# A hybrid encoder layer on one core: one rule for the PSUM banks of successive blocks, and other numbers of plain row blocks at the front of five blocks

## The chip, the cores and the metric

The kernel runs on one core of a Trainium2 chip. The metric is the device time of one execution in microseconds; before the change the median of three runs is 1933.54 (1931.85 to 1934.7). A profile is one more execution, taken by the hardware profiler; its span goes from the first to the last instruction.

## The reference, cut to what matters

One layer for 256 tokens of width 4096, all in float32. Cut to its shape:

```python
proj = rms_norm(x, g_mix) @ w_in                 # 4096 x 11840, split into eight parts
y_a = latent_attention(q latent, kv latent, rotary key) # 16 heads, dense softmax
y_a = rms_norm(y_a, g_out_mla) * silu(gate_a)
y_b = dilated_mixture_attention(q_b, k_b, v_b)   # 16 heads, ALiBi, three patterns
y_b = rms_norm(y_b, g_out_dil) * silu(gate_b)
x = x + concat(y_a, y_b) @ w_out                 # 4096 x 4096
x = x + (p @ w_ple) * sigmoid(rms_norm(x, g_ple) @ w_ple_gate)   # 4096 x 4096
return rms_norm(x, g_final)
```

Nearly all of the work is in the three large weight matrices, each read once.

## The kernel before, in words

**Products.** Every float32 operand is split into two parts, `hi` and `lo`, that TensorE takes in a faster format, and each product is the sum of three matmuls: activations `hi` by weights `hi` (L133), `hi` by `lo` (L134), `lo` by `hi` (L135). So L134 is the first that needs the weights' `lo`. The activations stand transposed in SBUF (tiles `A...`, `B...`, `T...`) and are loaded into the array, the weights stream through it. A product's result of 128 tokens by 512 columns fills one of the eight PSUM banks, named `m0` to `m3`, `s`, `o`, `t0`, `t1`.

**Weights.** SyncE issues the transfers of weight rows (L796 and L1339) into four `raw` buffers. ScalarE makes `hi` (L115), VectorE makes `lo` (L116), into a ring of tiles: three of the pool `wp` and, by block, one to three tiles that are free at that time (`B4`, `B6`, `Ah2`, ...). A step's conversion begins when the step that last used its ring place has run.

**Blocks.** A weight slice of 1024 columns by 4096 rows is a `Block` (class at L769). It works on two tiles of 128 tokens and two halves of 512 columns. A row block of 128 weight rows is either *plain* (`plain_step`: four products into the banks `M2`, `X`, `M3`, `M4`, 12 matmuls), or two row blocks together form a *fast group* after Strassen and Winograd (`fast_steps`: seven products instead of eight, 21 matmuls, into `M1`, `M2`, `M3`, `M5`, `M7`, `M6`, `M4`, in four steps). The fast groups need extra sums and differences of the operands: VectorE subtracts weights for them (L820) and converts the results (L116, L835). When the last fast group has run, a `mid` task reads the banks `M1`, `M6`, `M7`, `M5`; when the whole block has run, a `done` task reads `M2`, `X`, `M3`, `M4`. Eight banks serve one block, so the next block's first plain row block begins in banks that the `mid` task has read, if the tags are chosen so.

**Which banks.** `tags` gives a block's banks in the order `M2, X, M3, M4, M1, M5, M6, M7` (`Block.NAMES`). Before the change three orders are written out by hand: `EVEN`, `ODD` and `LAST`, and one more for the second block of the dilated group.

**The order of steps.** `weave(fast, lead, trail)` writes the order of a block: `lead` plain row blocks, then each fast group with the other plain row blocks spread among the groups, then `trail` plain row blocks. With `n` groups, 32 - 2n - lead - trail plain row blocks stand within. `lay` appends these steps to one list. The main loop goes through this list; for each step it issues the conversions some steps ahead, runs the step's matmuls, spawns the step's task, and lets every running task go one `yield` further (`advance`). Each engine executes its instructions in the order so written. Small jobs (transposes with their evacuation, attention heads, statistics) are such tasks; they take a bank for transposes by `turn_bank`, in turn from a list that `only` sets.

**The sequence.** Four chunks of the latents (banks by `banks()`, which alternates between `m0, m1` and `m2, m3`); the gate block (first group, 7 fast groups); the rest of that gate with the latent attention's up projections; six blocks of the dilated group's q, k, v; four gate chunks beside the dilated attention; three wide output blocks (`WIDE_O`, 4, 7 and 6 fast groups) and two output chunks; three wide blocks of the last gate (6, 7 and 7 fast groups) and the last chunks.

**Output blocks.** `out_done` (L922) adds the last four banks to the residual (L927), and then, after two yields, squares the result and turns it (`x1_turn`, L726): four transposes into one bank (L734), a yield, and `split_rows`, which reads that bank with ScalarE (L125) and VectorE (L127); four such sets a block. The banks for the turning are `t0, t1` during the first output block, `m0, m1` during the second, `m2, m3` during the third.

**The dilated group.** `d_mid` reads with L676 and L673, `d_done` with L691. **The last gate.** `wide_done` adds the last four banks (L1031) and then works by yields on its quarters: tanh on ScalarE (L1035), two VectorE instructions (L1038, L1039), a square on ScalarE (L1042). **The latents.** `done_a` of the fourth chunk computes the statistics (L357 to L362 and `rsqrt_mean`, L223 to L231) by yields during the gate block.

Of the kernel before, what the change touches and what calls it, by code (L numbers as in the profile page):

```python
# [29 lines left out]
OFF_GA = Q_LORA + KV_LORA + ROPE  # L30
# [48 lines left out]
def encoder_layer(ctx: ExitStack, tc: tile.TileContext, x, p, positions, g_mix, w_in, g_q_latent, w_uq,  # L79
# [3 lines left out]
    x, p, out = x[0], p[0, 0], out[0]  # L83
# [222 lines left out]
    T7 = {}  # L306
# [350 lines left out]
    def d_mid(key, blk):  # L657
        def task():
            tags = D_TAGS[key]
            if len(tags) == 2:  # L660
                d = [slot(b, [NT, 512]) for b in tags]
            else:
                both = slot(tags[0], [2, NT, 512])
                d = [both[:, 0], both[:, 1]]
            D[key] = d
            if key == ("v", 1):
                E["d"] = slot("T5", [2, NT, S])
                nc.gpsimd.dma_start(E["d"], c_dist)
            ps = blk.ps
            sc = [(rxq if key[0] == "q" else rx)[:, t:t + 1] for t in range(NT)]  # L670

            def add(h, t, m, old):
                nc.vector.scalar_tensor_tensor(d[h][:, t], ps[m], sc[t], old, op0=ALU.mult, op1=ALU.add)  # L673

            for t in range(NT):
                nc.scalar.activation(d[0][:, t], ps["M1"], AF.Copy, scale=sc[t])  # L676
            for t in range(NT):
                add(1, t, "M6", d[0][:, t])
            add(0, 1, "M7", d[1][:, 1])
            add(1, 0, "M5", d[1][:, 0])  # L680
            add(1, 1, "M5", d[0][:, 1])
            flags.add(("mid", key))
            yield
        return task

    def d_done(key, blk):
        def task():
            d = D[key]
            sc = [(rxq if key[0] == "q" else rx)[:, t:t + 1] for t in range(NT)]
            for m, t, h in (("M2", 0, 0), ("X", 1, 1), ("M3", 0, 1), ("M4", 1, 0)):  # L690
                nc.vector.scalar_tensor_tensor(d[h][:, t], blk.ps[m], sc[t], d[h][:, t], op0=ALU.mult, op1=ALU.add)  # L691
            if key == ("v", 1):
                E["t"] = slot("T4", [2, NT, S])
                for h in range(HEADS):
                    waiting.append((set(), attend(
                        h, lambda t, h=h: d_cols("q", h)[:, t], lambda t, h=h: d_cols("k", h)[:, t], None,
                        d_cols("v", h), yb_rows(h), True), 2 + h % 2))
                spawn(y_stats(1))
                spawn(split_ya())
            yield  # L700
        return task
# [54 lines left out]
    WP = ["wp"] * 3  # L756
# [165 lines left out]
    def out_done(k, blk):  # L922
        def task():
            quarters = ((0, 0, "M2"), (1, 1, "X"), (0, 1, "M3"), (1, 0, "M4"))
            for t, h, m in quarters:
                xc = x1[2 * k + h][:, t]
                nc.vector.tensor_tensor(xc, xc, blk.ps[m], op=ALU.add)  # L927
            yield
            yield
            turns_ = [x1_turn(2 * k + h) for h in range(2)]  # L930
            for h in range(2):
                for t in range(NT):
                    c = 2 * k + h
                    nc.scalar.activation(junk, x1[c][:, t], AF.Square, accum_out=ss1[:, t, c:c + 1])
                yield from turns_[h]
        return task
# [202 lines left out]


    M = ("m0", "m1"), ("m2", "m3")
    turn = [0]

    def banks():
        turn[0] ^= 1
# [13 lines left out]
    for i in range(4):  # L1159
        add(from_x(400 * i, 400, done_a(i)))  # L1160
    hooks = {}
    EVEN, ODD = ("m0", "m1", "s", "o", "m2", "m3", "t0", "t1"), ("m2", "m3", "t0", "t1", "m0", "m1", "s", "o")
    LAST = "m2", "m3", "s", "o", "m0", "m1", "t0", "t1"

    def weave(fast, lead, trail, e=0):

        n = len(fast)
        inner, out, given = 32 - 2 * n - lead - trail, "c" * lead, 0  # L1170
        for i in range(n):
            k = inner * (i + 1) // n - given
            given += k
            out += "c" * (k - 1) + "s" + "c" * (k > 0) + "sss"
        out += "c" * trail
        if e:
            out = out[:len(out) - trail + e] + "ee" + out[len(out) - trail + e:]
        rest = [kt for kt in range(32) if kt // 2 not in fast]
        return [("fast", j) for j in fast] + [("plain", kt) for kt in rest], out

    def lay(blk, order, mid, done, ple=None, after=(), used={}):

        pairs, shape = order
        step = {"s": iter([x for kind, j in pairs if kind == "fast" for x in blk.fast_steps(j)]),
                "c": iter([x for kind, kt in pairs if kind == "plain" for x in blk.plain_step(kt)]), "e": iter(ple or ())}
        last = shape.rindex("s")
        for i, key in enumerate(shape):
            x = next(step[key])
            x.ring = WP + list(after) if after != () and i > last else blk.ring
            if key == "s":  # L1190
                x.flag = used.get(shape[:i + 1].count("s") / 4)
            if i == last:
                x.after = mid
            if i == len(shape) - 1:
                x.after = done
            steps.append(x)

    def hook(at, f):
        assert at not in hooks
        hooks[at] = f  # L1200
# [6 lines left out]
    x0_s, z0 = {}, {}  # L1207
# [9 lines left out]
    def x_pair(j):  # L1217
# [1 line left out]

    hook(24, lambda: spawn(add_sums(7, x_pair, z0_dst, ("T2", "T3"), "x0_sums", x0_s, 2)))  # L1220
    gated_rings = {("T4", "T7"): ("used", 5), "B4": ("gated", 2), "Al1": ("y_sums", FAST_O - 1), ("T5", "T6"): "kpe"}
    order = weave(range(7), 6, 2)
    blk = Block(w_in[:, OFF_GA:OFF_GA + 1024], lhs_x, x0_s, "x0_sums", order, lambda kt: (), LAST, ("T2", "T3"),
                WP + [("T5", "T6")])
    lay(blk, order, gates_mid(blk), gates_done(blk))
    ga2 = from_x(OFF_GA + 1024, 512, done_gate(0, 2))
    ga2.banks, other = M
    for i in range(8):
        add(ga2, 2 * i, 2 * i + 1)
        add(Chunk(cols(w_uq, 384 * i, 384), 8, 384, lhs_c("q"), other, done_uq(i), lambda j: ["latents"]))  # L1230
# [2 lines left out]
    hook(len(steps), lambda: spawn(y_stats(0)))  # L1233
    hook(len(steps) + 1, lambda: spawn(x_sums()))
    ga3 = from_x(OFF_GA + 1536, 512, done_gate(0, 3))
    ga3.banks = M[0]
    add(ga3)

    x_s = {}
# [2 lines left out]
    def x_sums():  # L1242
# [5 lines left out]
            yield  # L1248
        yield from add_sums(8, x_pair, z, "B0", "x_sums", x_s, first=7)

    for n, key in enumerate((key, i) for i in range(2) for key in "qkv"):
        off = {"q": OFF_Q, "k": OFF_K, "v": OFF_V}[key[0]] + 1024 * key[1]
        order = weave((range(5), range(8), range(8), range(8), (4, 5, 0, 1, 2, 3, 6, 7), (0, 1, 2, 3, 6, 7))[n],
                      16 if n == 0 else 2, 2)
        ring = (["B6", "B4"], ["B4", "B6", "B0"], ["B4", "B6", "B0"], ["B4", "B6"], ["B4", ("T4", "T7")], [("T4", "T7")])[n]
        after = ((), (), ["B4", "B6"], ["B4"], [("T4", "T7")], ())[n]
        tags = LAST if n == 0 else ("t0", "t1", "m2", "m3", "m0", "m1", "s", "o") if n == 1 else (EVEN, ODD)[n % 2]
        blk = Block(w_in[:, off:off + 1024], lhs_x, x_s, "x_sums", order, lambda kt: (), tags, "B1", WP + ring)
        lay(blk, order, d_mid(key, blk), d_done(key, blk), after=after, used={2: ("used", 5)} if n == 4 else {})
    beside = [len(steps), len(steps) + 64]  # L1260
    for c in range(4):
        if c == 3:
# [2 lines left out]
        ch.banks = M[c % 2]  # L1265
        add(ch)

    for k in range(WIDE_O):
        hook(len(steps), only(*(("t0", "t1"), ("m0", "m1"), ("m2", "m3"))[k]))
        for h in range(2):  # L1270
            hook(len(steps) + 4 + h, lambda c=2 * k + h: load_res(c))
        order = weave(*((range(4), 12, 4), (range(7), 4, 4), (range(6), 6, 4))[k])
        blk = Block(w_out[:, 1024 * k:1024 * (k + 1)], lhs_y, y_s, "y_sums", order, lambda kt: need_y(kt // 2),
                    (EVEN, ODD)[k % 2], "Al2" if k < 2 else "Al1", WP + (["Ah2", "Al1"] if k < 2 else [("B7b", "T7")]))
        lay(blk, order, out_mid(k, blk), out_done(k, blk))
    for c in (6, 7):
        hook(len(steps), lambda c=c: (load_res(c), only("t0", "t1")()))
        if c == 7:
            hook(len(steps) + 6, lambda: spawn(x1_sums()))
            hook(len(steps) + 11, lambda: spawn(load_p()))  # L1280
        add(Chunk(cols(w_out, 512 * c, 512), 32, 512, lhs_y, ("m2", "m3") if c == 6 else ("m0", "m1"), done_o(c), need_y))
# [5 lines left out]
                     lambda j: ["pT"])  # L1287

    for k in range(WIDE):
        order = weave(*((range(6), 6, 4) if k == 0 else (range(7), 6, 4)), 2)  # L1290
        blk = Block(w_ple_gate[:, 1024 * k:1024 * (k + 1)], lhs_x1, x1_s, "x1_sums", order,
                    lambda kt: [("x1T", kt // 4)], LAST, "B6", WP + ["B4"])
        lay(blk, order, wide_mid(k, blk), wide_done(k, blk), wide_ple(k))
# [226 lines left out]
```

## Time and profile before

| | |
|---|---|
| median of three runs | 1933.54 us |
| the profiled execution | 1934.57 us |
| its span | 1932.8 us |
| granted TensorE clock | 0.997 |
| VectorE busy | 1560.3 us (81%) |
| ScalarE busy | 1103.9 us (57%) |
| weights' transfers, SyncE's queue | 363.90 MB, 61.5% of the 16 engines' time |

Blocks in the trace, by their first and last plain row block's matmuls: the gate block 156.6 to 241.8, the first two blocks of the dilated group from 491.5 and 580.0, the three output blocks from 1207.3, 1292.7 and 1381.6, the wide blocks of the last gate from 1557.0, 1647.5 and 1736.3.

How to read it: PE is TensorE's matmuls, PEld its weight loads, DVE VectorE, ACT ScalarE, SP SyncE. A timeline row has the start, the duration, the engine, the line, the operation, what it writes and reads, and in brackets how long the engine was idle before it and who ended that. The duration of a matmul is from its start to its modelled end; the next one starts earlier. `L116 ... lo<-raw,hi 128x1024` is the conversion of one row block.

### The profile page before, as it was taken

How to read it: one execution, taken by the hardware profiler on the slowest of the kernel's cores; microseconds unless marked ns; L12 is line 12 of the kernel's file. 1: busy time of each engine (PE TensorE's matmuls, PEld its weight loads, DVE VectorE, ACT ScalarE, POOL GpSimd, SP SyncE). 2: the span in 40 equal slices, each digit the busy share in tenths (PEclk: the TensorE clock that was granted, in tenths of full speed). 3: DMA queues.
4: the chain of work that ended last, by engine and by line, in shares of the span. 5: the costliest groups of instructions: out<-in, count | busy, mean ns of one | idle time of the engine just before them, and what ended most of it. 6: DMA issues, size and time to landing. Idle time of an engine off the chain costs nothing.

```text
span 1932.8 us, 25582 instructions
## 1 busy us (share of the span) xinstructions
PE 1909.9 (99%) x9272; PEld 1626.4 (84%) x9272; DVE 1560.3 (81%) x2162; ACT 1103.9 (57%) x1513; POOL 74.4 (4%) x122
## 2 busy tenths in 40 slices
PE   9999999999999999999999999999999999999997
PEld 8998889998887888888888888887888888888887
DVE  7767966666999999999877778888886688989866
ACT  6555565564655555655556666555555455656543
POOL 1001011220000000000000000000000000000000
PEclk9999999999999999999999999999999999999999
DMA  7666655545666666666665456665666656666675
GB/s 252 189 185 191 201 172 146 148 144 163 192 188 207 198 217 196 209 201 197 213 195 143 132 165 222 207 207 163 222 192 221 189 185 217 191 204 198 208 221 178
DMA packets 147342, 370.59 MB, mean 192 GB/s; under 512 B 12020, under 2 KB 45904, under 8 KB 147216
## 3 DMA queue, kind: packets, MB, share of 16 engines
q1 hardware_dynamic: 145584, 363.90, 61.5%
q0 software_dynamic: 1632, 5.05, 0.7%
q8 instruction: 73, 1.20, 0.3%
q14 instruction: 53, 0.43, 0.1%
HBM read 364.72 MB, written 4.19 MB: 191 GB/s over the span
## 4 chain that ended last, share of the span: by engine, by line
PE 91%; DVE 6%; ACT 1%; DMA 1%; issue 1%; SPq 0%; ACTq 0%; DVEq 0%
PE m L134 20%; PE m L135 19%; PE m L133 19%; PE t L133 3%; PE t L134 3%; PE t L135 3%; PE o L134 3%; PE o L135 3%; PE o L133 3%; PE s L134 3%; PE s L135 3%; PE s L133 3%; DVE lo L116 2%; DVE B L820 1%; DVE B L116 1%
## 5 line engine op out<-in xcount | busy, mean ns | idle before, releaser
L116 DVE TENSOR_TENSOR lo<-raw,hi 128x1024 fp32r<-128x1024 f32 (+4 forms) x502 | 552.1, 1105 | 230.4 <-ACT hi L115 227.6
L115 ACT ACTIVATE hi<-raw 128x1024 fp32r<-128x1024 f32 (+4 forms) x502 | 482.5, 965 | 379.4 <-PE m L135 158.6
L133 PE MATMUL m<-hi,Ah 128*128 128x512 f32 (+2 forms) x1113 | 422.3, 379 | 2.6 <-DVE B L691 1.5
L134 PE MATMUL m<-lo,Ah 128*128 128x512 f32 (+2 forms) x1113 | 417.2, 375 | 0.8 <-DVE lo L116 0.8
L135 PE MATMUL m<-hi,Al 128*128 128x512 f32 (+2 forms) x1109 | 414.6, 374 | 0.0
L133 PEld LDWEIGHTS m<-hi,Ah 128*128 128x128 f32 x1113 | 209.4, 188 | 32.6 <-DVE B L691 2.0
L134 PEld LDWEIGHTS m<-lo,Ah 128*128 128x128 f32 x1113 | 209.5, 188 | 32.4 <-DVE lo L116 3.7
L135 PEld LDWEIGHTS m<-hi,Al 128*128 128x128 f32 x1109 | 208.5, 188 | 32.4 <-DVE Al L127 0.2
L133 PE MATMUL m<-hi,B 128*128 128x512 f32 (+1 forms) x418 | 160.0, 383 | 2.8 <-DVE Al L127 2.8
L134 PE MATMUL m<-lo,B 128*128 128x512 f32 (+1 forms) x418 | 156.5, 374 | 0.2 <-DVE lo L116 0.2
L135 PE MATMUL m<-hi,B 128*128 128x512 f32 (+1 forms) x418 | 156.4, 374 | 0.0
L115 ACT ACTIVATE hi<-B 128x1024 fp32r<-128x1024 f32 x77 | 81.3, 1060 | 83.5 <-DVE B L820 55.2
L116 DVE TENSOR_TENSOR lo<-B,hi 128x1024 fp32r<-128x1024 f32 x77 | 93.8, 1221 | 5.3 <-ACT hi L115 2.8
L133 PEld LDWEIGHTS m<-hi,B 128*128 128x128 f32 x418 | 78.7, 188 | 13.6 <-issue 3.1
L115 ACT ACTIVATE B<-raw 128x1024 fp32r<-128x1024 f32 (+1 forms) x66 | 61.3, 938 | 47.9 <-DMA raw<-in_w_in_dram 18.2
L135 PEld LDWEIGHTS m<-hi,B 128*128 128x128 f32 x418 | 78.8, 188 | 11.7
L134 PEld LDWEIGHTS m<-lo,B 128*128 128x128 f32 x418 | 78.9, 189 | 11.5 <-DVE lo L116 1.0
L820 DVE TENSOR_TENSOR B<-raw,B 128x512 f32<-128x512 f32 x126 | 86.1, 683 | 0.0
L116 DVE TENSOR_TENSOR B<-raw,B 128x1024 fp32r<-128x1024 f32 (+1 forms) x66 | 70.4, 1074 | 16.6 <-ACT B L115 16.5
L116 DVE TENSOR_TENSOR T<-t,T 128x512 fp32r<-128x512 f32 (+1 forms) x65 | 44.4, 683 | 41.6 <-ACT T L115 41.2
L115 ACT ACTIVATE B<-B 128x1024 fp32r<-128x1024 f32 (+1 forms) x58 | 55.5, 957 | 36.6 <-DVE B L820 15.6
L835 DVE TENSOR_TENSOR lo<-raw,hi 128x1024 fp32r<-128x1024 f32 x56 | 68.2, 1218 | 3.6 <-ACT hi L833 3.6
(798 smaller groups left out, 3795.9 us busy)
## 6 DMA issues: line engine op xcount, KB each, us to landing
raw<-in_w_in_dram SPq DMA_DIRECT2D x320, 512.0 KB, 4.0
raw<-in_w_out_dram SPq DMA_DIRECT2D x128, 512.0 KB, 4.5
raw<-in_w_ple_gate_dram SPq DMA_DIRECT2D x128, 512.0 KB, 4.5
raw<-in_w_in_dram SPq DMA_DIRECT2D x63, 400.0 KB, 3.6
raw<-in_w_uq_dram SPq DMA_DIRECT2D x32, 384.0 KB, 3.4
raw<-in_w_ukv_dram SPq DMA_DIRECT2D x16, 512.0 KB, 3.8
T<-in_x_dram SPq DMA_DIRECT2D x7, 512.0 KB, 6.1
T<-in_x_dram POOLq DMA_DIRECT2D x7, 512.0 KB, 7.4
```

The source lines that it names most:

```text
L115: nc.scalar.activation(hi, src, AF.Copy)
L116: nc.vector.tensor_tensor(lo, src, plain(hi), op=ALU.subtract)
L133: nc.tensor.matmul(ps, ah, bh, start=start, stop=False)
L134: nc.tensor.matmul(ps, ah, bl, start=False, stop=False)
L135: nc.tensor.matmul(ps, al, bh, start=False, stop=stop)
L820: nc.vector.tensor_tensor(dst, a, b, op=ALU.subtract)
L835: nc.vector.tensor_tensor(lo, r[1], plain(hi), op=ALU.subtract)
```

## The change

Four things, with no instruction added or taken away:

- A block's banks come from the block in front by one rule, `follow`: the new `M2, X, M3, M4` are the old `M1, M6, M7, M5`, in the order in which the old block's `mid` task reads them; the new `M1, M5, M6, M7` are the old `M2, X, M4, M3`. The dilated group's six blocks and the three output blocks start from `EVEN` and follow on.
- The gate block takes `EVEN` instead of `LAST`, and `banks()` starts with the other pair, so that the `m` banks swap names up to the dilated group.
- `weave`'s lead: the gate block 8 instead of 6, the second output block 6 instead of 4, the third 8 instead of 6, the second and third wide block of the last gate 4 instead of 6.
- `out_done` has one yield less between the additions and the turning.

```diff
@@ out_done
             yield
-            yield
             turns_ = [x1_turn(2 * k + h) for h in range(2)]
@@
-    turn = [0]
+    turn = [1]
@@
-    EVEN, ODD = ("m0", "m1", "s", "o", "m2", "m3", "t0", "t1"), ("m2", "m3", "t0", "t1", "m0", "m1", "s", "o")
+    EVEN = "m0", "m1", "s", "o", "m2", "m3", "t0", "t1"
@@
+    def follow(tags):
+
+        m2, x, m3, m4, m1, m5, m6, m7 = tags
+        return m1, m6, m7, m5, m2, x, m4, m3
@@
-    order = weave(range(7), 6, 2)
-    blk = Block(w_in[:, OFF_GA:OFF_GA + 1024], lhs_x, x0_s, "x0_sums", order, lambda kt: (), LAST, ("T2", "T3"),
+    order = weave(range(7), 8, 2)
+    blk = Block(w_in[:, OFF_GA:OFF_GA + 1024], lhs_x, x0_s, "x0_sums", order, lambda kt: (), EVEN, ("T2", "T3"),
@@
-    ga2.banks, other = M
+    other, ga2.banks = M
@@
-    ga3.banks = M[0]
+    ga3.banks = M[1]
@@
+    tags = EVEN
     for n, key in enumerate((key, i) for i in range(2) for key in "qkv"):
...
-        tags = LAST if n == 0 else ("t0", "t1", "m2", "m3", "m0", "m1", "s", "o") if n == 1 else (EVEN, ODD)[n % 2]
         blk = Block(w_in[:, off:off + 1024], lhs_x, x_s, "x_sums", order, lambda kt: (), tags, "B1", WP + ring)
         lay(blk, order, d_mid(key, blk), d_done(key, blk), after=after, used={2: ("used", 5)} if n == 4 else {})
+        tags = follow(tags)
@@
+    tags = EVEN
     for k in range(WIDE_O):
...
-        order = weave(*((range(4), 12, 4), (range(7), 4, 4), (range(6), 6, 4))[k])
+        order = weave(*((range(4), 12, 4), (range(7), 6, 4), (range(6), 8, 4))[k])
         blk = Block(w_out[:, 1024 * k:1024 * (k + 1)], lhs_y, y_s, "y_sums", order, lambda kt: need_y(kt // 2),
-                    (EVEN, ODD)[k % 2], "Al2" if k < 2 else "Al1", WP + (["Ah2", "Al1"] if k < 2 else [("B7b", "T7")]))
+                    tags, "Al2" if k < 2 else "Al1", WP + (["Ah2", "Al1"] if k < 2 else [("B7b", "T7")]))
         lay(blk, order, out_mid(k, blk), out_done(k, blk))
+        tags = follow(tags)
@@
-        order = weave(*((range(6), 6, 4) if k == 0 else (range(7), 6, 4)), 2)
+        order = weave(*((range(6), 6, 4) if k == 0 else (range(7), 4, 4)), 2)
```

## Prediction

> **What bounds the kernel now.** I read the page's head first, then the waits of TensorE (engine, line, whom it waited for: total us, times, longest us), then the timeline around each of those waits.
>
> ```profile
> span 1932.8 us, 25582 instructions
> PE 1909.9 (99%) x9272; PEld 1626.4 (84%) x9272; DVE 1560.3 (81%) x2162; ACT 1103.9 (57%) x1513; POOL 74.4 (4%) x122
> PE m L133 <- DVE Al L127: 2.8, 1, 2.8
> PE m L133 <- DVE B L691: 1.5, 1, 1.5
> PE m L134 <- DVE B L116: 1.3, 2, 0.7
> PE m L134 <- DVE lo L116: 1.0, 4, 0.4
> PE m L134 <- DVE T L116: 0.6, 1, 0.6
> ```
>
> TensorE is busy for all but 22.9 us, and the change takes no matmul away. So only its waits can go, and these five rows sum to 7.2 us. The busy column hides part of what a wait costs, because a matmul's row (0.39) is longer than the distance between two starts. So I count from start to start:
>
> ```profile
> 1304.60 0.60 PE L734 MATMUL m<-ident,T 128*128 128x128 f32 x4
> 1308.04 0.47 PE L133 MATMUL m<-hi,B 128*128 128x512 f32 x1 [2.85 <-DVE Al L127]
> ...
> 1310.43 0.63 PE L133 MATMUL m<-hi,B 128*128 128x512 f32 x1
> 1310.86 0.63 PE L134 MATMUL m<-lo,B 128*128 128x512 f32 x1
> ...
> 1313.13 0.39 PE L134 MATMUL t<-lo,B 128*128 128x512 f32 x1
> 1313.36 0.40 PE L135 MATMUL t<-hi,B 128*128 128x512 f32 x1
> ```
>
> The undisturbed distance of 512-column matmuls is 0.23 (1313.13 to 1313.36; 0.2266 as a mean over many). Behind the 2.85 us wait eight of them stand 0.43 apart (1310.43 to 1310.86): the array ran at about half speed. A plain row block (4 banks, 12 matmuls) is thus 2.72 us, a fast group (21 matmuls) 4.76, a group with one plain row block in it 7.48.
>
> **The change part by part.**
>
> *Second output block (k = 1): one yield less, six plain row blocks ahead instead of four.* Its first fast product takes bank m0, in which the block in front still turns its result. The four transposes at 1304.60 are that block's third set; the product is issued right behind them and waits until ScalarE and VectorE have read the bank: 3.0 us more than 0.2 between the starts, 1.6 for eight matmuls 0.2 late, 0.2 for the edges: **4.8 us**. With the yield gone the third set stands behind the third plain row block (the order of the changed kernel's instructions shows it), and the product behind the sixth. Three plain row blocks, 8.2 us, lie between; the read took 3.1 (1304.9 to 1308.0). The wait goes whole. What takes its place? The first transposes now follow one plain row block after the last products, 1292.7 + 2.7 = 1295.4, and need the last addition to the result:
>
> ```profile
> 1292.72 0.39 PE L133 MATMUL m<-hi,B 128*128 128x512 f32 x1
> 1292.92 0.69 DVE L927 TENSOR_TENSOR T<-T,o 128x512 f32<-128x512 f32 x1
> ```
>
> It ends at 1293.6, 1.8 us early. The same holds for the other two output blocks. So -4.8. The Trainium skill, "TensorE: Matmul & The Clock Gate", section "Part 1: The HAM clock gate", has the array fall to half clock after at least one idle window of about 3.4 us, and 426.7 ns from start to start there. Those eight distances agree with its rate; a gap of 2.85 us would not fill its window, and by the rule taken strictly the term would be 3.2. The trace shows the slow stretch after this gap, so the rows stand.
>
> *The bank rule at the second block of the dilated group.*
>
> ```profile
> 581.17 0.39 PE L135 MATMUL t<-hi,Al 128*128 128x512 f32 x1
> 583.10 0.50 PE L133 MATMUL m<-hi,Ah 128*128 128x512 f32 x1 [1.53 <-DVE B L691]
> ...
> 582.30 1.40 DVE L691 SCALAR_TENSOR_TENSOR B<-m,st,B 128x512 f32<-128x512 f32 x2
> 584.93 1.21 DVE L116 TENSOR_TENSOR B<-raw,B 128x1024 fp32r<-128x1024 f32 x1
> ```
>
> The third bank of this block's first plain row block was m2, which the block in front fills until its end; VectorE reads it only at 582.3. By the new rule the first four banks are those that were read at the half-way task, done before 580. 1.7 us and 0.1 behind it go: **-1.8**. VectorE works through here without a pause, so what it delivers doesn't come earlier, and the next deadline moves up: the plain row block inside the first fast group is due at 580.04 + 5.44 + 0.68 + 0.23 = 586.4, and its conversion (584.93 + 1.21) ends at 586.15. That just holds; if it is late, by some tenths. At all other block edges of this stretch no wait is listed, and the new rule reads the same four early banks in another order: 0. That the m-banks swap names in front of it changes no distance: 0.
>
> *Gate block of the first group: eight ahead instead of six, so 8 instead of 10 plain row blocks within the seven groups.*
>
> ```profile
> 172.08 1.23 DVE L116 TENSOR_TENSOR lo<-raw,hi 128x1024 fp32r<-128x1024 f32 x1 [2.12 <-ACT hi L115]
> 182.76 1.23 DVE L116 TENSOR_TENSOR T<-raw,T 128x1024 fp32r<-128x1024 f32 x1
> 183.90 0.15 DVE L229 SCALAR_TENSOR_TENSOR st<-st 128x4 f32<-128x4 f32 x1
> ...
> 181.68 0.39 PE L133 MATMUL m<-hi,Ah 128*128 128x512 f32 x1
> 182.43 0.50 PE L134 MATMUL m<-lo,Ah 128*128 128x512 f32 x1 [0.36 <-DVE lo L116]
> ...
> 183.00 0.40 PE L133 MATMUL m<-T,Ah 128*128 128x512 f32 x1
> 184.04 0.50 PE L134 MATMUL m<-T,Ah 128*128 128x512 f32 x1 [0.65 <-DVE T L116]
> ```
>
> The starts lose 0.5 and 0.8, with edges 1.5 us. VectorE is late because the latent's statistics (some 17 small instructions, 2.7 us) fall among its first group. With two more plain row blocks in front, its queue is: conversion of the sixth ends at 173.3 as now, 1.1 for the turned latents, 1.8 for the subtractions and half conversion, 1.1 for the next plain row: 177.3. One group of VectorE there is 7.54 (four subtractions at 0.6, a half conversion at 0.6, four conversions at 1.13) and the statistics 2.7: the second group's plain row is ready at 187.6. TensorE would have wanted it at 184.04 less the 1.5 of waits, and wants it two plain row blocks later: 188.0. After that VectorE needs 7.54 a group against 7.48: level. Here the price is the denser stretch, bounded below by 0 and above by the denser blocks' rows further down (up to 0.9 in one group, so some 1.5). I take 0.1: **-1.4**.
>
> *Wide blocks 1 and 2 of the last gate: four ahead instead of six, 10 instead of 8 within.*
>
> ```profile
> 1702.06 0.39 PE L133 MATMUL m<-B,Ah 128*128 128x512 f32 x1
> 1703.02 0.50 PE L134 MATMUL m<-B,Ah 128*128 128x512 f32 x1 [0.57 <-DVE B L116]
> ...
> 1790.86 0.40 PE L133 MATMUL m<-B,Ah 128*128 128x512 f32 x1
> 1791.97 0.50 PE L134 MATMUL m<-B,Ah 128*128 128x512 f32 x1 [0.71 <-DVE B L116]
> ...
> 1687.31 1.21 DVE L835 TENSOR_TENSOR lo<-raw,hi 128x1024 fp32r<-128x1024 f32 x1
> 1695.14 1.22 DVE L835 TENSOR_TENSOR B<-raw,B 128x1024 fp32r<-128x1024 f32 x1
> 1694.65 5.89 DMA raw<-in_w_ple_gate_dram
> ```
>
> VectorE's group takes 7.83 here (L835 to L835), TensorE's 7.48, so each group loses 0.35, until the fourth and fifth stand still; a weight transfer of 5.89 adds to it. That is 1.0 and 1.2 us. With 10 inside, three groups hold two plain row blocks (10.2 of TensorE) and the loss goes. But the first group now starts 5.4 us earlier, beside the last steps of the block in front:
>
> ```profile
> 1648.26 2.35 DVE L116 TENSOR_TENSOR lo<-raw,hi 128x1024 fp32r<-128x1024 f32 x2
> 1652.66 0.68 DVE L1038 SCALAR_TENSOR_TENSOR B<-B,Q 128x512 f32<-128x512 f32 x1
> 1653.38 0.69 DVE L1039 TENSOR_TENSOR T<-B,T 128x512 f32<-128x512 f32 x1
> ```
>
> Four such pairs, 1.3 to 1.4 each, now stand between the group's conversions. From 1650.6, when the lead is converted: 1.8 for the subtractions, 1.3, until 1654.5 for a transfer, then five conversions (1.14 each), two subtractions (0.6) and three pairs: 1664.3 for the fourth step, due 1664.7. Then 0.5 (the pause before a group's first subtraction in these rows), 1.8, 1.1: 1667.8 against 1666.8. So about 1.0 us of wait comes back, bounds 0 and 1.6 (every pair also late by its own ScalarE input). Net **-0.2** for both.
>
> *Third output block (eight ahead), and the second one's denser middle (8 inside instead of 10 in both).*
>
> ```profile
> 1332.62 1.23 DVE L116 TENSOR_TENSOR lo<-raw,hi 128x1024 fp32r<-128x1024 f32 x1 [0.25 <-ACT hi L115]
> 1336.26 0.39 PE L134 MATMUL m<-lo,B 128*128 128x512 f32 x1
> ```
>
> In the second output block a plain row inside a group is ready 2.4 us ahead of its use (1333.85 to 1336.26), the closest that I found there, since its ring has five places. Five groups at a loss of 0.35 use up 1.8 of it; one slow transfer more uses up the rest. The third output block has two groups in a row at most. I take +0.2, bounds 0 and 1.5.
>
> Sum: -4.8 - 1.8 - 1.4 - 0.2 + 0.2 = **-8.0 us**. The profiled execution took 1934.57 in all (1932.8 of span), 1.0 above the median of the three runs (1933.54): 1926.6 on its own scale, 1925.5 on the median's. I give **1925.6**.
>
> **The rivals.**
> - *The dense middles cost more than the lead gives.* For it: VectorE's 7.83 against 7.48 shows in the rows above, and the removed 4.8 us were also time for VectorE to catch up. In each of the gate block, the second and the third output block up to 1.5 us comes back, and 0.6 more in each wide block: gain 8.0 - 4.5 - 1.2, about 2.5 to 5; 1929 to 1931. Against it: the margins worked out above.
> - *The wide blocks come clean too* (the pairs find gaps): 2.2 instead of 0.2, and nothing at the third output block: gain about 10.2, 1923.3.
> - *Slower.* Mechanism: without the yield the first transposes stand one plain row block behind the last products. If the last addition (L927) ends over 2.7 us after the block's start, TensorE waits there, at three edges. If the wait reaches the 2.85 us of the row above, the half-speed stretch comes with it: 4.8 each, 14.4 in all, less 8.0: 1940. It decides from 1.8 us more delay of that addition; L927 runs 0.9 after the start, and nothing is moved in front of it in VectorE's order.
> - *The rule doesn't do what it says* (a first bank read last somewhere): the 1.8 stays and a second edge like it costs 1.8: 1929.
>
> **How the numbers follow.** The forecast (gain 6.5 to 9.5) 0.55, dense middles 0.19, clean wide blocks 0.13, rule fails 0.07, slower 0.06. The range reaches from a gain of 11 (10.2 and the spread of runs) to one of 3.5: 1922.5 to 1930; it leaves out the slower case and the worst of the dense one. A measurement of this kernel tells about 0.2%, 3.9 us. All cases but the slower and some half of the dense one gain more: faster 0.85, same 0.10, slower 0.05.
>
> **What would show it.** In the changed profile: no wait on L127 and no matmuls 0.43 apart at the second output block; no wait on L691 (its new line) at 580; at 180 to 190 no wait above 0.3; in the wide blocks the wait moves from the fifth group to the second, about 1 us. Wrong would be waits at L734's transposes, growing waits on L116 late in the gate block or the second output block, or a span not shorter by the sum of the waits that went.

## The result and the profile after

The changed kernel takes 1927.40 us (median of 7 runs, 1926.62 to 1928.79); the kernel before, run between them on the same chip, 1933.64 (7 runs). The ratio is 0.997 (95% interval 0.9958 to 0.9981): 6.2 us or 0.3% faster. A second series gave 1927.74 against 1933.52, ratio 0.997 (0.9959 to 0.9981). The execution that was profiled took 1927.64 us. The head of its page and the waits of TensorE (engine, line, whom it waited for: total us, times, longest us):

```profile
span 1925.9 us, 25586 instructions
PE 1909.8 (99%) x9272; PEld 1626.7 (84%) x9272; DVE 1560.8 (81%) x2162; ACT 1101.3 (57%) x1513; POOL 74.5 (4%) x122
```

```profile
PE m L1456 <- DVE junk L1450: 1.5, 1, 1.5
PE m L134 <- DVE lo L116: 0.9, 5, 0.2
PE t L270 <- DMA T<-in_x_dram: 0.9, 1, 0.9
PE t L169 <- DMA T<-in_g_mix_dram: 0.2, 1, 0.2
```

The four instructions more than before (25582) are semaphore instructions, three on VectorE and one on TensorE; the counts of each engine's work are the same.

The waits on L127 (2.8) and L691 (1.5) have no row left, those on L116 fell from 2.9 to 0.9. What stays is at the kernel's start, which no edit aims at, and five small waits of L134. TensorE's busy time moves by 0.1 us only; what went is its idle time, 22.9 us before and 16.1 after.

To see where the time went I cut TensorE's timeline at the first product of each block, and took the distance to the first product of the next one. Every number of a block below is such a length. Before and after, us:

```
                                         before    after    difference
kernel start up to the gate block        156.64   157.19    +0.55
gate block, first group                   85.19    84.21    -0.98
second block of the dilated group         83.42    81.63    -1.79
second output block                       88.87    84.26    -4.61
last gate, second wide block              88.79    88.69    -0.10
last gate, third wide block               88.95    88.59    -0.36
last chunk to its end                     35.46    35.78    +0.32
the 15 others, together                                     +0.04
```

The third output block, whose lead and banks the change alters too, is among the 15: 84.94 before, 84.95 after. The edits bought nothing there.

At the second output block, TensorE's timeline of the changed kernel (start us, length, engine, line, out<-in) shows the third set of transposes and what stands behind it:

```profile
1302.91 0.60 PE L734 MATMUL m<-ident,T 128*128 128x128 f32 x4
1303.26 0.48 PE L133 MATMUL m<-hi,B 128*128 128x512 f32 x1
...
1312.23 0.39 PE L133 MATMUL m<-Al,B 128*128 128x512 f32 x1
1312.46 0.39 PE L134 MATMUL m<-Al,B 128*128 128x512 f32 x1
```

Three plain row blocks follow the set, and nine microseconds on the distance is still 0.23: neither the wait nor the stretch of 0.43 exists. At the start of the second dilated block:

```profile
581.41 0.39 PE L135 MATMUL t<-hi,Al 128*128 128x512 f32 x1
581.63 0.39 PE L133 MATMUL m<-hi,Ah 128*128 128x512 f32 x1
...
583.84 0.74 DVE L691 SCALAR_TENSOR_TENSOR B<-o,st,B 128x512 f32<-128x512 f32 x1
584.50 1.22 DVE L116 TENSOR_TENSOR B<-raw,B 128x1024 fp32r<-128x1024 f32 x1
585.72 0.39 PE L133 MATMUL m<-B,Ah 128*128 128x512 f32 x1
585.94 0.39 PE L134 MATMUL m<-B,Ah 128*128 128x512 f32 x1
```

L691 still reads the old block's banks at 583.8, but the new block's first four banks are others, and TensorE takes the fourth at 581.63 without a gap. The next plain row is met with little to spare: its conversion (L116) ends at 585.72, and the product that needs it starts at 585.94, 0.22 behind the one in front.

In the wide blocks the wait moved to the second group. Before it stood in the fifth and, for the most part, in the sixth, counted from one (the prediction calls them the fourth and fifth):

```profile
1659.06 0.40 PE L133 MATMUL m<-hi,Ah 128*128 128x512 f32 x1
1659.64 0.50 PE L134 MATMUL m<-lo,Ah 128*128 128x512 f32 x1 [0.18 <-DVE lo L116]
1660.20 0.40 PE L133 MATMUL m<-hi,Ah 128*128 128x512 f32 x1
1660.77 0.50 PE L134 MATMUL m<-lo,Ah 128*128 128x512 f32 x1 [0.17 <-DVE lo L116]
```

### The profile page after: what moved, and what is told of

Same layout as the page of the kernel before. It is cut to its first block, busy times and chain, and to the rows that moved or that the text cites. A ratio compares the mean times of both kernels' runs of the same rounds, so it can differ in the third digit from the quotient of the medians.

```text
span 1925.9 us, 25586 instructions
## 1 busy us (share of the span) xinstructions
PE 1909.8 (99%) x9272; PEld 1626.7 (84%) x9272; DVE 1560.8 (81%) x2162; ACT 1101.3 (57%) x1513; POOL 74.5 (4%) x122
## 4 chain that ended last, share of the span: by engine, by line
PE 94%; DVE 4%; DMA 1%; issue 1%; ACT 1%; SPq 0%; DVEq 0%; ACTq 0%
PE m L134 20%; PE m L135 20%; PE m L133 20%; PE t L134 4%; PE t L135 4%; PE t L133 4%; PE s L134 3%; PE o L134 3%; PE o L135 3%; PE o L133 3%; PE s L135 3%; PE s L133 3%; DVE lo L116 1%; PE t L445 1%; DVE B L820 1%
## 5 line engine op out<-in xcount | busy, mean ns | idle before, releaser
L116 DVE TENSOR_TENSOR lo<-raw,hi 128x1024 fp32r<-128x1024 f32 (+4 forms) x497 | 549.0, 1109 | 227.6 <-ACT hi L115 225.0
L133 PE MATMUL m<-hi,Ah 128*128 128x512 f32 (+2 forms) x1130 | 429.2, 380 | 0.0
L134 PE MATMUL m<-lo,Ah 128*128 128x512 f32 (+2 forms) x1130 | 424.6, 376 | 0.9 <-DVE lo L116 0.7
L135 PE MATMUL m<-hi,Al 128*128 128x512 f32 (+2 forms) x1128 | 422.3, 374 | 0.0
L134 PEld LDWEIGHTS m<-lo,Ah 128*128 128x128 f32 x1130 | 212.9, 188 | 34.6 <-DVE lo L116 5.0
L134 PE MATMUL m<-lo,B 128*128 128x512 f32 (+1 forms) x420 | 156.8, 373 | 0.2 <-DVE lo L116 0.2
L135 PE MATMUL m<-hi,B 128*128 128x512 f32 (+1 forms) x420 | 156.7, 373 | 0.0
L116 DVE TENSOR_TENSOR lo<-B,hi 128x1024 fp32r<-128x1024 f32 x75 | 91.6, 1223 | 4.1 <-ACT hi L115 1.8
L134 PEld LDWEIGHTS m<-lo,B 128*128 128x128 f32 x420 | 79.1, 188 | 11.3 <-DVE lo L116 0.9
L116 DVE TENSOR_TENSOR B<-raw,B 128x1024 fp32r<-128x1024 f32 (+1 forms) x66 | 69.4, 1059 | 13.5 <-ACT B L115 13.2
L116 DVE TENSOR_TENSOR T<-t,T 128x512 fp32r<-128x512 f32 (+1 forms) x65 | 44.4, 683 | 41.6 <-ACT T L115 41.2
```

What stands on the lines that cost most here:

```text
L116: nc.vector.tensor_tensor(lo, src, plain(hi), op=ALU.subtract)
L133: nc.tensor.matmul(ps, ah, bh, start=start, stop=False)
L134: nc.tensor.matmul(ps, ah, bl, start=False, stop=False)
L135: nc.tensor.matmul(ps, al, bh, start=False, stop=stop)
```

## Experiments

My theory: the gain is three waits that went, each by its own edit, and the wide blocks gain next to nothing. Against it stood that the edits need each other, that they only move VectorE's delay to another place, and that the output blocks' edges are at the point of tipping over. The tables name lengths as above.

**The lead of the second output block alone** (on the kernel before):

```diff
-        order = weave(*((range(4), 12, 4), (range(7), 4, 4), (range(6), 6, 4))[k])
+        order = weave(*((range(4), 12, 4), (range(7), 6, 4), (range(6), 6, 4))[k])
```

> The kernel before, with only the second output block's lead changed from four plain row blocks to six; both yields stay. My theory: the third set of transposes stays behind the fourth plain row block, the first fast product goes behind the sixth, so 5.4 us of plain work lies where the read of the bank took 3.1: the wait on L127 (2.85 us before) and the eight matmuls 0.43 apart both go, and the block shortens by the whole 4.8 us (88.87 to about 84.0). The rival, that the yield's removal is what frees the bank and the lead only adds cover, has most of the wait left: under 2 us gained. All other blocks unchanged.

Measured: 1929.48 us against 1934.14, ratio 0.9976 (0.9967 to 0.9986). The second output block takes 84.26, to the hundredth what both edits give. Its banks are the old ones here, so the rule in the output blocks adds nothing to this.

**The yield alone** (on the kernel before):

```diff
@@ out_done
             yield
-            yield
             turns_ = [x1_turn(2 * k + h) for h in range(2)]
```

> The kernel before, with only one yield taken out of the output block's end task; the second output block keeps its lead of four. The third set of transposes then stands behind the third plain row block and the first fast product behind the fourth: 2.7 us of plain work for a read of about 3.1. My theory: a wait of 0.2 to 0.5 us on L127 stays, too short to be followed by matmuls 0.43 apart, so the block shortens by 4.2 to 4.6 us. The rival, that any wait at this place brings the half-speed stretch, gives 2.8 to 3.2 us. A second rival, that the two edits each carry half of the gain and must come together: about 2.4.

Measured: 1929.45 us, ratio 0.9977 (0.9967 to 0.9987); the block is again 84.26. Not even the small wait came that I expected:

```profile
1301.57 0.60 PE L734 MATMUL m<-ident,T 128*128 128x128 f32 x4
...
1304.00 0.87 DVE L127 SCALAR_TENSOR_TENSOR Al<-m,gT,Ah 128x256 fp32r<-128x256 f32 x2
1304.79 0.60 PE L734 MATMUL m<-ident,T 128*128 128x128 f32 x4
1305.14 0.48 PE L133 MATMUL m<-hi,B 128*128 128x512 f32 x1
```

The read ends at 1304.87, 3.3 us behind the set's start. The first fast product is due at 1305.14, since the fourth set of transposes (0.35) stands between as well; I had left that out. So either edit takes the whole wait, and the two aren't halves of one gain: in the changed kernel one of them is spare.

**The bank rule alone** (the rule in the six dilated blocks, started from the banks that the first of them has before):

```diff
+    tags = LAST
     for n, key in enumerate((key, i) for i in range(2) for key in "qkv"):
...
-        tags = LAST if n == 0 else ("t0", "t1", "m2", "m3", "m0", "m1", "s", "o") if n == 1 else (EVEN, ODD)[n % 2]
...
+        tags = follow(tags)
```

> The kernel before, with only the bank rule in the six dilated blocks (each block's banks follow from the block in front, starting from the banks that the first of them has already). My theory: the 1.5 us wait of the second dilated block on L691 goes, its length falls from 83.42 to about 81.6 (1.8 us), and no other dilated block changes by over 0.1. The rival, that the 1.8 us in the changed kernel came from the swapped names of the banks in front of the group and not from the rule, leaves 83.4 here.

Measured: 1933.45 us, ratio 0.9995 (0.9986 to 1.0005). The second dilated block falls to 81.60 as expected; but the four chunks behind the group rise from 215.99 to 217.13. There stands the same kind of wait:

```profile
990.41 0.39 PE L135 MATMUL m<-hi,Al 128*128 128x512 f32 x1
991.61 0.50 PE L133 MATMUL m<-hi,Ah 128*128 128x512 f32 x1 [0.81 <-DVE B L691]
```

The first chunk's second bank is one that the sixth block filled last.

**The rule with the swapped names** (all bank edits in front of and in the dilated group; leads, yields and output blocks as before):

> The kernel before with all edits of banks in front of and in the dilated group (the rule, its start, the swapped names), but with leads, yields and the output blocks as before. My theory of the 1.1 us that appeared behind the last dilated block when the rule stood alone: the rule alternates two sets of first banks, and with the old names it ends on the set that the next chunk takes, so the swapped names belong to it. Then here the second dilated block is 81.6, the chunks behind the group are back at 216.0, and the time is 1.8 us under before, 1932.3. Rival: the 1.1 us come from the rule whatever its start: 217.1 and 1933.4.

Measured: 1932.24 us against 1934.64, ratio 0.9987 (0.9977 to 0.9996); second dilated block 81.65, chunks behind the group 216.00. The gate block, whose banks change here but not its lead, stays at 85.17. So the swap isn't decoration: the rule hands banks on from block to block, and where it starts decides what the chunk behind the last block finds.

**One yield more taken away** (on the changed kernel):

```diff
-            yield
             turns_ = [x1_turn(2 * k + h) for h in range(2)]
```

> The changed kernel, with the output block's second yield taken out as well, so that the first set of transposes stands directly behind the block's last products at all three edges. My theory: the transposes then wait for the last addition (L927 ended 0.9 us after the next block's start), and the bank that they turn in is wanted by the next block's second to fourth product, 0.7 to 2.0 us later, while reading it takes about 3: a wait of 2 to 4 us at each of the three edges, 8 to 14 us in all with half-speed stretches, 1935 to 1941. The rival, that nothing but the bank of the second edge limits these edges and the transposes may stand anywhere: within 1 us of the changed kernel.

Measured: 1945.17 us (1944.28 to 1946.06), 17.8 above the changed kernel and more than I expected. The three output blocks and the first output chunk, the four stretches around the three edges, grow by 1.25, 6.86, 3.50 and 6.25. The first edge:

```profile
1289.75 0.27 PE L734 MATMUL t<-ident,T 128*128 128x128 f32 x1
1290.69 0.55 PE L734 MATMUL t<-ident,T 128*128 128x128 f32 x3 [0.67 <-DVE T L927]
...
1291.54 0.40 PE L135 MATMUL m<-hi,B 128*128 128x512 f32 x1
1295.73 0.76 PE L133 MATMUL t<-hi,B 128*128 128x512 f32 x1 [3.79 <-DVE Al L127]
1296.29 0.63 PE L134 MATMUL t<-lo,B 128*128 128x512 f32 x1
1296.71 0.63 PE L135 MATMUL t<-hi,B 128*128 128x512 f32 x1
```

The wait on the last addition is only 0.67. The bank that the set turns in costs the rest: the second product behind the set wants it and waits 3.79, and half speed follows. The third edge is alike (3.79); at the second the wait is 2.41, without half speed. The rival on record for "slower" had TensorE waiting at the transposes for the last addition. That wait is real here but small; what makes this kernel slow is the bank, which the rival doesn't name. One plain row block in front of the first set keeps the changed kernel clear of both.

**Leads, two sets** (on the changed kernel; gate block / first wide block / second and third wide block / first dilated block: 7, 8, 5, 13 and 9, 7, 3, 15, instead of 8, 6, 4, 16):

> The changed kernel with other leads in four blocks, each read by its own length. Gate block 7 instead of 8: the second group's plain row falls due 2.7 us earlier, part of the old wait returns: 84.2 becomes 84.5 to 85.2. First block of the last gate 8 instead of 6: its two waits of about 0.45 go, 90.4 becomes 89.6. Second and third block of the last gate 5 instead of 4: my theory that the wait of the second group (0.9 us) comes from the four pairs of the block in front says that 2.7 us more time frees it: 88.6 to 88.7 becomes 87.8. Rival: the wait is the loss of 0.35 a group and depends on the number inside alone, so it comes back in a later group: 88.4 to 88.9. First dilated block 13 instead of 16: two groups with two plain row blocks inside take up the loss, 88.55 becomes 87.7; rival: the sums of the lhs come too late for groups that start 8 us earlier, over 89. All together: 2 to 3 us under the changed kernel, about 1925.

> The changed kernel with leads moved the other way, each block read by its own length. Gate block 9 instead of 8: one plain row block in every group, so the three waits of 0.2 in the later groups stay: 84.0 to 84.3. First block of the last gate 7 instead of 6: half of its 0.9 goes, 90.0. Second and third block of the last gate 3 instead of 4: if the four pairs set the wait of the second group, it grows by up to 2.7 us: 89.5 to 91.4 each; by the rival (loss per group alone, here with 11 plain row blocks inside) it goes: 87.8. First dilated block 15 instead of 16: one plain row block in every group: 88.0 to 88.3. All together 1 to 5 us above the changed kernel, by the rival 2 below.

```
                          6 (before)      7              8              9
gate block                85.2            83.84          84.2 to 84.8   83.84
first wide block          90.4 to 91.0    89.39          89.4
                          3               4              5              6
second and third wide     88.85 88.78     88.7 and 88.7  88.3 and 88.3  88.5 and 88.6
```

Where more kernels share a lead, the table gives their range or their mean (five kernels at 6, three at 4, two at 5 in the wide blocks, whose length strays by 0.6 from kernel to kernel at the same lead). The first set took 1925.10 us (ratio 0.9951, 0.9936 to 0.9966), the second 1927.05 (0.9961, 0.9946 to 0.9976). I was wrong on several points. In the gate block already one more plain row in front takes the old waits away, so my working has the second group's plain row ready over a microsecond too late; and nine ahead gives 83.84, not 84.0 to 84.3. In the first wide block, too, one more in front is as good as two: 89.39, not 90.0. Three ahead in the second and third wide block costs 0.1, not up to 2.7 as by my theory, and they don't fall to 87.8 as by the rival. Five ahead gains 0.4, half of what my theory says. The first dilated block doesn't care (88.40 and 88.55 against 88.55), where I expected 87.7 and 88.0 to 88.3. So the first set's total came as expected, and the second set's is 0.4 under the changed kernel, not 1 to 5 above. The first wide block, which the change leaves alone, had 1.0 us to give.

**The four pairs later, and without them.** First the tanh steps of the wide blocks, and with them the pairs on VectorE, eight steps later:

```diff
-            yield
+            for _ in range(9):
+                yield
             for n in range(6):
                 for i, t, h, m in quarters[n:n + 1]:
```

> The changed kernel, in which the tanh steps of the last gate's wide blocks, and with them the four pairs on VectorE, start eight steps later; leads stay at four. If the pairs between the first group's conversions make the second group's wait (0.35 twice with edges, 0.9 us in each of the two blocks), it goes, and both blocks fall from about 88.65 to 87.8, unless a later group takes it over: 1.7 us in all, 1925.7. If the wait is the loss of VectorE's 7.83 against 7.48 a group, it stays: within 0.3 us of the changed kernel.

Measured: 1933.59 us. The two blocks grow to 91.11 and 91.95, neither of the two lengths that I had named: the wait leaves the second group's place and comes back larger in the third, where VectorE works through without a pause and the four pairs stand between its conversions.

```profile
1671.44 0.40 PE L133 MATMUL m<-B,Ah 128*128 128x512 f32 x1
1673.32 0.50 PE L134 MATMUL m<-B,Ah 128*128 128x512 f32 x1 [1.49 <-DVE B L116]
```

Then the pairs left out, at four ahead and at six (one profiled execution each):

```diff
-                    nc.vector.scalar_tensor_tensor(u, u, 1.0, P4[t, h], op0=ALU.add, op1=ALU.mult)
-                    nc.vector.tensor_tensor(xc, u, xc, op=ALU.add)
+                    pass
```

> The changed kernel (four ahead in the second and third block of the last gate) without the four pairs on VectorE: it leaves out the gate's product with the embedding and its addition in six of the nine column blocks. My theory, two reserves: with four ahead the wait of the second group comes from the pairs, which eat VectorE's reserve at the block's start; without them no wait over 0.15 us is left in either block, and each falls from 88.2 to 88.9 (the scatter seen) to 87.6 to 87.9. Rival, the loss of 0.35 us a group alone: the wait stays, 88.2 or more.

> The same without the pairs, with six ahead in these two blocks, as in the kernel before. My theory: here the pairs are done long before the wait of the fourth and fifth group, and conversions run only five steps ahead, so VectorE can't save up what the pairs leave; the loss of 0.35 us a group brings the same wait of 0.6 to 1.2 us at the fifth group, with or without pairs: 88.2 to 88.9. Rival, that the pairs' 5.4 us of work set the waits of both leads: 87.8 here too.

Measured: 87.72 and 87.89 with four ahead, where kernels with the pairs have 88.59 to 88.79; 88.31 and 88.30 with six, where kernels with the pairs have 88.29 to 88.95. At six the wait of the sixth group (the fifth in my count above) is still there, 0.22 and 0.11 over the distance of 0.23 (1695.52 to 1695.97 to 1696.31):

```profile
1695.52 0.39 PE L133 MATMUL m<-B,Ah 128*128 128x512 f32 x1
1695.97 0.50 PE L134 MATMUL m<-B,Ah 128*128 128x512 f32 x1
1696.31 0.40 PE L135 MATMUL m<-B,Al 128*128 128x512 f32 x1
```

So both are true: with four ahead the pairs make the wait; with six a wait stays without them, as the steady loss of a group has it. At the block's start the lead gives VectorE the time to do the pairs; done later, they find no such time.

**The leads together, and the changed kernel once more:**

> The changed kernel with leads 7 (gate block, instead of 8), 8 (first block of the last gate, instead of 6) and 5 (second and third block, instead of 4); the first dilated block stays at 16. From the blocks' lengths measured with these leads: 0.4 and 1.0 less, and 0.4 less in each of the two last (those by a scatter of 0.6): 2.2 us under the changed kernel, so some 9 us under before. The rival, that block lengths with other neighbours don't add: within 1 us of the changed kernel.

> The changed kernel once more, against more runs of before. By the sum of the blocks that the change touches it should be 7.4 to 7.8 us faster, unless its kernel start or end is longer for a reason of its own: in the first profile they took back 0.9. If that was scatter, its start (up to the gate block) comes out at 156.2 to 157.2 us as in the other kernels and its last block at 35.4 to 36.1.

The leads 7, 8 and 5 took 1926.12 us (ratio 0.9964, 0.9952 to 0.9977), 1.6 under the changed kernel's 1927.74 of the same series: the gate block 83.83, the wide blocks 89.39, 88.33 and 88.36. The lengths come as measured singly; the total gains a little less than their 2.2.

The changed kernel's repeat is 5.8 us faster than before, not the 7.4 to 7.8 that I expected. Its start (157.18) and its last block (35.48) came out as in the other kernels; its profile, of the slowest of the seven executions (1928.98), is longer in two blocks.

This profile is the most telling of all, since the kernel is the same: its gate block took 84.77 instead of 84.21, its second output block 85.15 instead of 84.26. Timeline of ScalarE and VectorE in the second output block, first profile and then the repeat:

```profile
1320.17 1.06 ACT L115 ACTIVATE Ah<-raw 128x1024 fp32r<-128x1024 f32 x1 [1.33 <-DMA raw<-in_w_out_dram]
...
1321.42 1.22 DVE L116 TENSOR_TENSOR Ah<-raw,Ah 128x1024 fp32r<-128x1024 f32 x1
```

```profile
1322.56 1.06 ACT L115 ACTIVATE Ah<-raw 128x1024 fp32r<-128x1024 f32 x1 [3.11 <-DMA raw<-in_w_out_dram]
...
1323.65 1.23 DVE L116 TENSOR_TENSOR Ah<-raw,Ah 128x1024 fp32r<-128x1024 f32 x1 [1.54 <-ACT Ah L115]
...
1340.16 0.40 PE L133 MATMUL m<-Ah,B7a 128*128 128x512 f32 x1
1340.62 0.50 PE L134 MATMUL m<-Ah,B7a 128*128 128x512 f32 x1
...
1348.00 0.40 PE L133 MATMUL m<-Ah,B7a 128*128 128x512 f32 x1
1348.46 0.50 PE L134 MATMUL m<-Ah,B7a 128*128 128x512 f32 x1
```

One weight transfer came late, VectorE stood still for 1.54, and two groups later the plain rows of two groups are met 0.23 late (with edges some 0.35 each). In the gate block the same happens on a smaller scale: ScalarE waits 1.88 for a weight transfer where it waited 1.11 in the first profile, and VectorE stands still at 218.28:

```profile
218.28 1.23 DVE L116 TENSOR_TENSOR lo<-raw,hi 128x1024 fp32r<-128x1024 f32 x1 [0.43 <-ACT hi L115]
```

## Why the prediction was right, point by point

- *Second output block, -4.8.* Measured -4.61 in every profile of a kernel with one of these edits or both, but the repeat's (-3.72) and the kernel with neither yield. The mechanism is as told: the transposes' bank, read in 3.1 to 3.3, behind three plain row blocks instead of none. What the prediction didn't see is that either edit alone does it.
- *Bank rule, -1.8.* Measured -1.76 to -1.82 in every kernel that has it, and the conversion behind it was in time, by 0.2.
- *Swapped names, 0.* They cost nothing at the blocks, and are needed: without them the rule gives back 1.1 us. The rival "the rule doesn't do what it says" was right as a mechanism, for another kernel. Up to the gate block, the four profiled kernels with the old names took 156.25 to 157.12 (mean 156.7), the ten with the new ones 156.48 to 157.92 (mean 157.3). The names don't matter once the kernel runs: from the 25th matmul of the weights' products on, some 15 us into the kernel, the way to the gate block is 142.16 to 142.21 in all fourteen. The scatter lies ahead of it, where TensorE waits for the first transfers and runs at half speed for a time that differs (matmuls of 400 columns stand 0.33 apart until 10.5 us in the profile after, and 0.18 from 7.6 on in the one before); the first of these matmuls starts at 7.17 to 8.59 with the old names and at 7.59 to 8.86 with the new ones. Whether the 0.6 between the means is more than chance is open; no run changed the names alone.
- *Gate block, -1.4.* Measured -0.98, in the repeat -0.42. The old waits went as told. Mis-sized was the price of the denser stretch, taken at 0.1 from bounds of 0 and 1.5: each of three later groups is some 0.2 late, edges included, 0.6 in all. So one of the signs of being wrong that the prediction names, waits on L116 late in the gate block, is there, though small. The rows of the first:

```profile
203.34 0.39 PE L133 MATMUL m<-T,Ah 128*128 128x512 f32 x1
203.63 0.50 PE L134 MATMUL m<-T,Ah 128*128 128x512 f32 x1
203.97 0.39 PE L135 MATMUL m<-T,Al 128*128 128x512 f32 x1
```

- *Wide blocks, -0.2.* The wait moved to the second group and is about 0.9, as told (0.35 and 0.34 over the distance, and edges of 0.11). The working names five conversions behind the transfer; its sum of 1664.3 is that of four, and four is what the trace after shows there. Of the net, one pair of profiles says -0.46; over five kernels with six ahead the two blocks sum to 177.2, over three with four ahead to 177.4. The term is 0 within the scatter of 0.6. Why three ahead costs no more was not followed up.
- *Denser output blocks, +0.2, bounds 0 and 1.5.* 0 in seven of the eight profiles with these leads, +0.9 in the repeat, by the late transfer that the prediction named.
- *Sum.* Block by block, as means over the profiles of kernels with these edits: -0.8 for the gate block, -1.8, -4.5, +0.2 for the wide blocks, and +0.6 at the start, which may be chance, together -6.3. The medians say -6.2 and -5.8. So 8.0 was 1.7 too high: 0.6 of it in the gate block, 0.1 in the output blocks (4.8 less 0.2, against 4.5), 0.4 in the wide blocks, and 0.6 at a start that I had taken as given.

Of the rivals, "dense middles" holds part of the truth: it acts in some executions and not in others, where I had it as one state of the kernel. Its gain of 2.5 to 5 would have needed the repeat's delays in every block.

## What to carry to other kernels

Before a bank is blamed on its place, work out how much work stands between its last write and its next use, and compare it with the time of the read: here 3.57 from the transposes to the product against a read of 3.3 was already enough, and a second remedy bought nothing. A rule that hands resources from stage to stage must be checked at its last stage too, where something that doesn't follow the rule takes over. A stage that an engine meets with nothing to spare shows its price only in some executions: compare more than one profile of the same kernel before a term is called 0.

## What the runs showed of the hardware

TensorE fell to half speed behind some of these waits and not behind others. The wait of 2.85 us had such a stretch in all three kernels that have the wait: the kernel before and the two with edits of the banks in front of the output blocks. In the kernel before the stretch begins about a microsecond behind the wait; with the rule alone, behind the same wait at the same place, at once:

```profile
1307.86 0.77 PE L133 MATMUL m<-hi,B 128*128 128x512 f32 x1 [2.85 <-DVE Al L127]
1308.42 0.63 PE L134 MATMUL m<-lo,B 128*128 128x512 f32 x1
1308.85 0.63 PE L135 MATMUL m<-hi,B 128*128 128x512 f32 x1
```

The block is as long in both (88.87 and 88.83): the stretch moves, and its cost stays. The Trainium skill, "TensorE: Matmul & The Clock Gate", section "Part 1: The HAM clock gate", describes a window of about 3.4 us that runs freely, so that the moment depends on where the work falls in it. The shifted start agrees with that, and the granted clock shows the window: in all fourteen profiles, every later change of the clock on record comes a whole number of steps of 3.41 us behind the first. Three such steps of the kernel before (first the stretch and its length, then the busy us of PE, PEld, DVE, ACT and POOL, then the granted clock):

```profile
1305.94:1309.35 3.41, 1.31 (x8) 1.17 (x9) 3.15 (x5) 0.98 (x3) 0.00 (x0) 1.00 0.00 0
1309.35:1312.76 3.41, 3.41 (x10) 2.64 (x9) 1.57 (x3) 1.01 (x3) 0.00 (x0) 0.50 0.31 85
1312.76:1316.18 3.42, 3.42 (x17) 2.81 (x16) 1.30 (x2) 2.09 (x2) 0.00 (x0) 1.00 0.17 68
```

A step with 2.10 us of idle is followed by one at clock 0.50, which costs 1.7 us of work, near the 1.6 that the prediction counted. It isn't the length of the wait that decides. In the kernel with neither yield the wait of 2.41 us falls on two steps, with 0.87 and 1.55 of idle, and the clock stays:

```profile
1386.85 0.47 PE L133 MATMUL m<-hi,B 128*128 128x512 f32 x1 [2.41 <-DVE Al L127]
```

```profile
1381.89:1385.30 3.41, 2.54 (x12) 1.81 (x12) 1.75 (x2) 3.30 (x6) 0.00 (x0) 1.00 0.00 0
1385.30:1388.72 3.42, 1.87 (x10) 1.63 (x11) 1.40 (x3) 0.91 (x1) 0.00 (x0) 1.00 0.76 235
1388.72:1392.13 3.41, 3.41 (x18) 2.84 (x17) 2.05 (x4) 3.34 (x9) 0.00 (x0) 1.00 0.43 136
```

In the first set of leads a wait of only 1.76 us at the kernel's start falls whole into one step (4.54 to 7.96), and the next step has the clock at 0.50. Of all such steps at full clock in the fourteen profiles, each with 1.88 us of idle or more is followed by half clock, and none with 1.73 or less is; of two in between, with 1.76 and 1.77, one is. So these traces put the point at about half a step of idle, counted step by step. No run was made to test this.
